# Two hybrid layers put in order by an older cost clock, and products that share the TensorE array issued with the last-ready operand first

## The chip, the cores and the metric

The kernel runs on one core of a Trainium2 chip. The metric is the device time of one execution in microseconds (us); less is better. The engines are PE (TensorE, whose weight loads are listed as PEld), DVE (VectorE), ACT (ScalarE), POOL (GpSimd) and SP (SyncE, which here issues the loads of the weights).

## What is computed

The reference passes 512 tokens of width 1024 through one block of RWKV-7 and S5 mixing with a gated feed-forward net, and then through two hybrid layers. Only the hybrid layers matter here. Cut to the core:

```
for l in range(2):
    h = rms_norm(x, norm_g)
    q_lat, kv_lat, k_rope, g_mla, c_h, c_b, c_c, g_conv, s_q, s_k, s_v, g_swa = split(h @ w_in)
    q = rms_norm(q_lat) @ w_qb               # MLA: 8 heads of 64 + 32 (the 32 with rope)
    k, v = rms_norm(kv_lat) @ w_kvb
    y_mla  = softmax(causal(q . k)) @ v * silu(g_mla)
    y_conv = c_b * conv3(c_c * c_h) * silu(g_conv)
    # 8 query heads, 2 key heads, window of 128, a slope and a sink for each head
    y_swa  = softmax(window(s_q . s_k) - slope * dist, sink) @ s_v * silu(g_swa)
    x = x + concat(y_mla, y_conv, y_swa) @ w_out
```

## The kernel before

Three parts follow one another on the core: the front (RWKV and S5), the feed-forward net, and the two hybrid layers, which take from about 838 us to the end: layer 0 to about 1215 us, layer 1 after it.

The large products are made in float32 precision from fp32r halves: each operand is split into `hi` (ACT, a copy to fp32r) and `lo` (the rest, DVE or POOL), and each product tile takes three matmuls, hi x hi, lo x hi and hi x lo. In the rows these are `mm<-hhi,whi`, `mm<-hlo,whi` and `mm<-hhi,wlo` where the input of the layer is multiplied, and `mm<-yhi,whi` and so on for `w_out`. `wraw` is a weight tile as it was loaded, `whi` and `wlo` are its halves. Small products and all transposes (`rp<-c,...`, against the identity in `c`) are of type float32.

Each layer is written as a set of Python generators, one for each strand of work: `mla_q`, `mla_k` and `swa_q` for queries and keys, `mla_s` to `mla_t` for MLA's scores, softmax and transposed probabilities (`P` in rows, `pt` in the layout for the value product), `mla_v` for the value products into `O`; `swa_s`, `swa_m`, `swa_e` and `swa_v` for the window attention (`P`, transposed into `wt`); `gated` multiplies `O` with the gate into `yt` and splits it into `yhi` and `ylo`. `sums` (L2207) adds squares for the key and query norms: four products with 32 columns of the array each (`rp<-sq,c`), one on each quarter of it, and four transposes of the result. Two products of 64 columns (`O<-pt,vt` and `O<-wt,vs`) also share the array, one for each head of a pair.

A scheduler, class `Flow`, runs while the kernel is built. At each step it asks every strand for its next operation, works out when that could start (`look`) and, from a cost model (`cost`), when its engine is free again, and issues the one with the least start time plus a bias for its strand (`turn`, `run`). `emit` issues it on the line L541, which is therefore the line of all operations that no helper issues, transposes among them. So the model's figures set the order of each engine's instructions; on the chip each engine works through its own list in that order and waits for operands by semaphores. The model has a table of latencies from engine to engine (`AFTER`), a price for changing between float32 and fp32r products on PE (`SWITCH`), and a rule that an operation of DVE with two SBUF operands and one of POOL do not run together (`ported`). The order in which weight loads stand on SP's queue comes from job lists, in the order of the products. `over` (in the body) is called when the last products of the feed-forward net have been issued, and starts the first hybrid layer.

Of the kernel before, what the change touches and what calls it, by code (L numbers as in the profile page):

```python
# [14 lines left out]
PSUM = bass.MemoryType.PSUM  # L15
# [362 lines left out]
class Flow:  # L378
# [9 lines left out]
    SWITCH = 0.06  # L388

    def __init__(self, tc):  # L390
        self.tc = tc
        self.free, self.log, self.slot, self.count = {}, {}, {}, {}
        self.live, self.now, self.last, self.beside = [], 0.0, {}, set()
        self.kind, self.ports = None, {"DVE": [], "Pool": []}
        self.table, self.psum = None, set()
        self.part, self.recent, self.ticks, self.urgent, self.late = None, [], {}, lambda: False, lambda: False
# [36 lines left out]
    def cost(eng, fn, out, args, kw=None):  # L433
        kw = kw or {}
        size = lambda ap: int(np.prod([c for _, c in ap.ap[1:]]))
        n, name = size(out), getattr(fn, "__name__", "")
        if eng == "PE":
            ins = [a for a in args if hasattr(a, "ap")]
            n, m = size(ins[-1]), size(ins[1])
            if ins[1].dtype == F32R:  # L440
                return (max(n, m) + 32) / 2400.0
            if name == "transpose":
                return n * 2 / 2400.0
            return 4 * max(n, m) / 2400.0
        psum = Flow.psums(args, kw)
        if eng == "ACT":
            return max(0.19, (0.165 if psum else 0.195) + n * 0.00085) + sum(
                c for k, c in (("accum_out", 0.19), ("bias", 0.08), ("scale", 0.08)) if hasattr(kw.get(k), "ap"))
        if name in ("reduce_sum", "tensor_reduce"):
            n = size(kw.get("in_", out))  # L450
        if eng == "DVE":
            rate = 2.0 if name == "tensor_tensor_scan" else 0.5 if not psum and name in ("TS", "memset", "tensor_copy") else 1.0
            return 0.15 + n * rate / 960.0 + (0.06 if n > 50 and (name == "tensor_tensor_reduce" or name in ("TS", "STT") and hasattr(args[2], "ap"))
                                              else 0.0)
# [5 lines left out]
    def ported(eng, fn, args, kw):  # L460

        name = getattr(fn, "__name__", "")
        if eng not in ("DVE", "Pool") or name in ("memset", "dma_start"):
            return False
# [22 lines left out]
    def look(self, o):  # L487
# [9 lines left out]
        for (key, p0, p1, f0, f1), w in boxes:  # L497
            for q0, q1, g0, g1, t, w2, e2 in self.log.get(key, ()):
                if (w or w2 or e2 != eng and key in self.psum) and p0 < q1 and q0 < p1 and f0 < g1 and g0 < f1:
                    if eng == "PE" and e2 == "PE" and (w and w2):  # L500
                        continue
                    start = max(start, t + (0.95 if e2 == "DMA" else self.AFTER.get((e2, eng), 0.2)))
        if not dma and self.ported(eng, fn, args, kw):
# [34 lines left out]
    def emit(self, o, plan):  # L538
# [11 lines left out]
        if eng == "PE":  # L550
            kind = args[1].dtype == F32R
            start, self.kind = start + (self.SWITCH if self.kind not in (None, kind) else 0.0), kind
        end = start + self.cost(eng, fn, out, args, kw) if not dma else start + (0.1 if eng != "Pool" else 1.05)
# [1356 lines left out]
class Layer:  # L1910
# [296 lines left out]
    def sums(self, ts, cols):  # L2207

        X, R, o = self.X, self.R, Flow.op
        ps = yield from R["rp"].take()  # L2210
        for j, t in enumerate(ts):
            yield o(X.MM, ps[32 * j:32 * j + 32], cols, t)
        R["sq"].free(*ts)
# [242 lines left out]
    def mla_v(self):  # L2456
        X, R, o, M = self.X, self.R, Flow.op, self.mla
        for h in range(0, 8, 2):
            yield lambda: 7 + h // 2 in self.gates
            O = yield from R["O"].take()  # L2460
            for c in range(4):
                yield lambda: ("t", h, c) in M and ("t", h + 1, c) in M
                for e in range(2):
                    pt, n, g = M.pop(("t", h + e, c)), (4 - c) * 128, (h + e) * 64
# [86 lines left out]
    def swa_v(self):  # L2551
        X, R, o, M = self.X, self.R, Flow.op, self.mla
        for pr in range(4):
            O = None
            for hf in range(2):
# [20 lines left out]
                for n, (qb, c) in enumerate(blocks):  # L2576
                    for e in range(2):
                        yield o(X.MM, O[64 * e:64 * e + 64, qb * 128:(qb + 1) * 128], self.vs[:, c, e * 64:(e + 1) * 64],
# [278 lines left out]
def second(X, top, tail, stop):  # L2857
# [21 lines left out]

    def over():  # L2880
        fst.close()
        lp, R["lt"], yp = [pool(top, n) for n in ("lp", "lt", "ly")]
# [39 lines left out]
```

## Time and profile before

| what | value |
| --- | --- |
| three runs | 1603.16, 1604.68, 1603.89 us (median 1603.89) |
| profiled execution | 1600.54 us, its span 1598.8 us |
| PE busy | 1505.8 us, 94% of the span |
| DVE, ACT, POOL busy | 868.5, 656.3, 531.0 us |
| granted TensorE clock, mean | 0.982 |

Busy means that an instruction of the engine was running. The span is the time from the first to the last instruction in the trace; the execution's own time is 1.7 us longer. In rows, `out<-in` names the output and input tiles, `xN` says how many instructions were taken together, and brackets say how long the engine had been idle ahead of the row and what released it.

### The profile page before, as it was taken

Reading aid. Unit: us, or ns where it says so; the run is one execution under the profiler, and the core shown is the slowest. Engines: PE = TensorE matmul, PEld = TensorE weight load, DVE = VectorE, ACT = ScalarE, POOL = GpSimd, SP = SyncE. Lnnn points to the kernel's source line nnn. Section 1 sums busy time; section 2 is a strip of 40 time slices with the busy share of each in tenths; the row PEclk is TensorE's granted clock in tenths of the full one; section 3 lists DMA queues with packets and bytes.
Section 4 is the critical chain, followed back from the end, with each engine's and each line's share of the span. In section 5 each row is a group of like instructions: output and inputs, shape, how many; then the busy total and the mean of one; then the engine's idle time right before and its main releaser. Section 6 shows DMA issues by size and latency. Waiting matters only on the chain. (4 is left out here: it accounts for less than half of the span.)

```text
span 1598.8 us, 23587 instructions
## 1 busy us (share of the span) xinstructions
PE 1505.8 (94%) x8772; PEld 1134.7 (71%) x8772; DVE 868.5 (54%) x2011; ACT 656.3 (41%) x1316; POOL 531.0 (33%) x498
## 2 busy tenths in 40 slices
PE   4998999998879999999999999999989999999988
PEld 2666677675458888888888777776768867766766
DVE  6858875784774222222234753547855574354872
ACT  3422533231243333333333664464544555355451
POOL 1111341221333333334433454522233454532221
PEclk9999999999989999999999999999989999999999
DMA  6773141323122322333322212221112312211212
GB/s 246 288 206 82 55 112 31 115 52 94 57 78 81 99 93 99 100 91 96 101 90 83 73 47 66 81 71 54 60 53 71 105 59 67 80 60 54 73 47 86
DMA packets 97684, 141.92 MB, mean 89 GB/s; under 512 B 40977, under 2 KB 44945, under 8 KB 97553
## 3 DMA queue, kind: packets, MB, share of 16 engines
q1 hardware_dynamic: 90512, 120.46, 24.9%
q0 software_dynamic: 5760, 18.88, 3.8%
q8 instruction: 69, 1.13, 0.3%
q10 hardware_dynamic: 1296, 1.07, 0.2%
q14 instruction: 47, 0.38, 0.1%
HBM read 135.39 MB, written 4.98 MB: 88 GB/s over the span
## 5 line engine op out<-in xcount | busy, mean ns | idle before, releaser
L236 POOL TENSOR_TENSOR wlo<-wraw,whi 128x512 fp32r<-128x512 f32 (+2 forms) x300 | 376.9, 1258 | 753.0 <-ACT whi L233 731.2
L233 ACT ACTIVATE whi<-wraw 128x512 fp32r<-128x512 f32 (+2 forms) x392 | 239.6, 613 | 448.8 <-PE mm L255 315.4
L255 PE MATMUL mm<-hhi,whi 128*128 128x512 f32 x920 | 369.8, 402 | 3.9 <-ACT vt L233 2.1
L255 PE MATMUL mm<-hhi,wlo 128*128 128x512 f32 x920 | 369.6, 402 | 3.3 <-DVE wlo L236 1.5
L255 PE MATMUL mm<-hlo,whi 128*128 128x512 f32 x920 | 368.3, 400 | 0.0
L255 PEld LDWEIGHTS mm<-hhi,wlo 128*128 128x128 f32 x920 | 175.6, 191 | 45.7 <-POOL wlo L236 4.2
L255 PEld LDWEIGHTS mm<-hhi,whi 128*128 128x128 f32 x920 | 175.4, 191 | 45.6 <-issue 7.2
L255 PEld LDWEIGHTS mm<-hlo,whi 128*128 128x128 f32 x920 | 175.7, 191 | 41.3 <-issue 6.1
L236 DVE TENSOR_TENSOR wlo<-wraw,whi 128x512 fp32r<-128x512 f32 (+1 forms) x92 | 64.7, 703 | 112.9 <-ACT whi L233 112.8
L255 PE MATMUL mm<-yhi,whi 128*128 128x512 f32 x224 | 92.8, 414 | 5.3 <-ACT yhi L233 5.3
L255 PE MATMUL mm<-ylo,whi 128*128 128x512 f32 x224 | 91.1, 407 | 1.7 <-POOL ylo L236 1.7
L255 PE MATMUL mm<-yhi,wlo 128*128 128x512 f32 x224 | 90.6, 405 | 0.0
L255 PE MATMUL mm<-ahi,whi 128*128 128x512 f32 x176 | 69.3, 394 | 0.0
L255 PE MATMUL mm<-ahi,wlo 128*128 128x512 f32 x176 | 69.0, 392 | 0.0
L255 PE MATMUL mm<-alo,whi 128*128 128x512 f32 x176 | 68.3, 388 | 0.0
L541 PEld LDWEIGHTS rp<-c,P 128*128 128x128 f32 x272 | 32.5, 140 | 36.6 <-issue 14.0
L541 DVE CUSTOM_DVE_ANT_0 P<-rp,c,nsq 128x128 f32<-128x128 f32 (+1 forms) x64 | 34.1, 550 | 43.2 <-PE rp L255 29.7
L236 DVE TENSOR_TENSOR xres<-xres,mm 128x512 f32<-128x512 f32 x48 | 32.7, 685 | 45.4 <-PE mm L255 45.1
L541 PE MATMUL rp<-c,P 128*128 128x128 f32 x272 | 47.4, 282 | 10.5 <-DVE P L249 10.3
L252 DVE SCALAR_TENSOR_TENSOR xres<-mm,ada,xres 128x512 f32<-128x512 f32 x40 | 29.7, 748 | 48.3 <-PE mm L255 48.0
L255 PEld LDWEIGHTS mm<-yhi,whi 128*128 128x128 f32 x224 | 43.2, 193 | 15.5 <-ACT yhi L233 6.5
L252 DVE SCALAR_TENSOR_TENSOR g<-th,mm 128x512 f32<-128x512 f32 x21 | 14.5, 688 | 70.5 <-PE mm L255 70.5
(548 smaller groups left out, 2656.7 us busy)
## 6 DMA issues: line engine op xcount, KB each, us to landing
wraw<-in_w2m SPq DMA_DIRECT2D x124, 256.0 KB, 2.7
wa<-in_wada SPq DMA_DIRECT2D x40, 512.0 KB, 5.1
wraw<-in_wo SPq DMA_DIRECT2D x48, 256.0 KB, 2.7
wraw<-in_wgate SPq DMA_DIRECT2D x44, 256.0 KB, 2.7
wraw<-in_wup SPq DMA_DIRECT2D x44, 256.0 KB, 2.8
wraw<-in_wdown SPq DMA_DIRECT2D x40, 256.0 KB, 2.7
wraw<-in_wz POOLq DMA_DIRECT2D x24, 256.0 KB, 3.2
wa<-in_wada POOLq DMA_DIRECT2D x8, 512.0 KB, 3.5
```

The costliest lines, as they stand in the source:

```text
L233: return self.act.activation(out=out, in_=in_, func=func, **kw)
L236: return (eng or self.dve).tensor_tensor(out=out, in0=a, in1=b, op=op)
L252: return self.dve.scalar_tensor_tensor(out=out, in0=a, scalar=s, in1=b, op0=op0, op1=op1)
L255: return self.pe.matmul(out, lhsT=lhsT, rhs=rhs, start=start, stop=stop)
L541: ins = fn(*args, **kw)
```

## The change

No instruction is added or taken out: each engine has as many as before, and SP's queue is the same. What differs is the order on PE, DVE, ACT and POOL, from the point at which `over` is called; the front and the feed-forward net up to there are as before. (1) `over` sets `Flow.rough`: from there the model uses a second table of latencies, `ROUGH`, an fp32r product without the 32 columns added, shorter ACT and DVE operations, no price for changing between float32 and fp32r, and no port rule. (2) `sums` issues its four products in reverse, the last operand first. (3) `mla_v` and `swa_v` issue the second head of a pair (`e` = 1) ahead of the first.

```diff
+    ROUGH = {("PE", "ACT"): 0.2, ("PE", "DVE"): 0.24, ("ACT", "DVE"): 0.15, ("DVE", "ACT"): 0.14, ("DVE", "DVE"): 0.125,
+             ("ACT", "ACT"): 0.2, ("DVE", "PE"): 0.2, ("ACT", "PE"): 0.25, ("PE", "PE"): 0.04}
+    rough = False
...
             if ins[1].dtype == F32R:
-                return (max(n, m) + 32) / 2400.0
+                return (max(n, m) + (0 if Flow.rough else 32)) / 2400.0
...
+        if Flow.rough and eng == "ACT":
+            return max(0.11, 0.06 + n * 0.00087) + sum(
+                c for k, c in (("accum_out", 0.1), ("bias", 0.12), ("scale", 0.08)) if hasattr(kw.get(k), "ap"))
...
+        if Flow.rough and eng == "DVE":
+            half = 0.5 if name in ("TS", "memset") or name == "tensor_copy" and "PSUM" not in str(args[1].tensor.space) else 1.0
+            return 0.067 + n * half / 960.0 + (0.06 if n > 50 and (name == "tensor_tensor_reduce" or name in ("TS", "STT") and hasattr(args[2], "ap"))
+                                               else 0.0)
...
-        if eng not in ("DVE", "Pool") or name in ("memset", "dma_start"):
+        if Flow.rough or eng not in ("DVE", "Pool") or name in ("memset", "dma_start"):
             return False
...
-                    start = max(start, t + (0.95 if e2 == "DMA" else self.AFTER.get((e2, eng), 0.2)))
+                    start = max(start, t + (0.95 if e2 == "DMA" else (self.ROUGH if Flow.rough else self.AFTER).get((e2, eng), 0.2)))
...
-            start, self.kind = start + (self.SWITCH if self.kind not in (None, kind) else 0.0), kind
+            start, self.kind = start + (self.SWITCH if self.kind not in (None, kind) and not Flow.rough else 0.0), kind
...
-        for j, t in enumerate(ts):
-            yield o(X.MM, ps[32 * j:32 * j + 32], cols, t)
+
+        for j in reversed(range(len(ts))):
+            yield o(X.MM, ps[32 * j:32 * j + 32], cols, ts[j])
...
                 yield lambda: ("t", h, c) in M and ("t", h + 1, c) in M
-                for e in range(2):
+
+                for e in (1, 0):
...
                 for n, (qb, c) in enumerate(blocks):
-                    for e in range(2):
+                    for e in (1, 0):
...
     def over():
+        Flow.rough = True
```

Three places show the new order. First PE in the first `sums` of layer 0; `rp_8023` (after: `rp_8026`) is the sum's tile, `kb` rows are transposes of MLA's keys. Before:

```order
L255 MATMUL rp_8023<-sq_7887,c_4357 32x512
L255 MATMUL rp_8023<-sq_7915,c_4357 32x512
L255 MATMUL rp_8023<-sq_7991,c_4357 32x512
L255 MATMUL mm_8007<-hhi,whi_7943 128x512
L255 MATMUL mm_8007<-hlo,whi_7943 128x512
L255 MATMUL mm_8007<-hhi,wlo_7944 128x512
...
L255 MATMUL rp_8023<-sq_8009,c_4357 32x512
L255 MATMUL mm_8007<-hhi,whi_7972 128x512
```

After:

```order
L255 MATMUL mm_8002<-hhi,wlo_7945 128x512
L553 MATMUL rp_7862<-c_68,yt_7842 128x128
L255 MATMUL rp_8026<-sq_8004,c_4357 32x512
L255 MATMUL rp_8026<-sq_7988,c_4357 32x512
L255 MATMUL rp_8026<-sq_7919,c_4357 32x512
L255 MATMUL rp_8026<-sq_7891,c_4357 32x512
L553 MATMUL rp_8040<-c_68,kb_8028 128x128 x4
L255 MATMUL mm_8002<-hhi,whi_7968 128x512
```

The six fp32r products that stood between the third and the fourth product of the sum (three of them are left out above) have moved, and the four stand in one piece.

Second, DVE at the end of layer 1: the softmax of the last half of the last head pair of the window attention (`wmn` its maximum, `wse` and `wrs` its sum, `P` the probabilities). Before:

```order
L236 TENSOR_TENSOR gate_13961<-mm_13860,rb 128x512
L541 TENSOR_REDUCE wmn<-sc_13819 128x4
L252 SCALAR_TENSOR_TENSOR gate_13961<-sq_13977,gate_13961 128x512
L236 TENSOR_TENSOR xres<-xres,mm_13960 128x512
L236 TENSOR_TENSOR wmn<-wmn,nsink 128x4
L236 TENSOR_TENSOR wmn<-wmn,c_4357 128x4
L236 TENSOR_TENSOR wse<-wmn,rows 128x4
L236 TENSOR_TENSOR wrs<-wrs,wse 128x4
L541 RECIPROCAL wrs<-wrs 128x4
L249 TENSOR_SCALAR P_14025<-P_14025,wrs 128x256 x4
```

After:

```order
L553 TENSOR_REDUCE wmn<-sc_13781 128x4
L236 TENSOR_TENSOR wmn<-wmn,nsink 128x4
L236 TENSOR_TENSOR wmn<-wmn,c_4357 128x4
L236 TENSOR_TENSOR wse<-wmn,rows 128x4
L252 SCALAR_TENSOR_TENSOR yt_13944<-O_13905,gate_13886 128x512
L236 TENSOR_TENSOR wrs<-wrs,wse 128x4
L553 RECIPROCAL wrs<-wrs 128x4
L249 TENSOR_SCALAR P_13948<-P_13948,wrs 128x256 x4
L236 TENSOR_TENSOR gate_13992<-mm_13885,rb 128x512
L252 SCALAR_TENSOR_TENSOR gate_13992<-sq_13996,gate_13992 128x512
```

The two steps of the gate and the addition to `xres` have moved from the middle of the softmax to behind it, and `yt` of the pair before has come into it.

Third, PE at the same place, from the last transposes of `P` to the first product with the last pair's `yhi`. Before:

```order
L255 MATMUL mm_14007<-yhi_13925,whi_13943 128x512
L255 MATMUL mm_14007<-ylo_13926,whi_13943 128x512
L255 MATMUL mm_14007<-yhi_13925,wlo_13944 128x512
L541 MATMUL rp_14039<-c_68,P_14025 128x128 x4
L541 MATMUL rp_14046<-c_68,P_14025 128x128 x4
L255 MATMUL O_13988<-wt_14044,vs 64x128
L255 MATMUL O_13988<-wt_14051,vs 64x128
...
L255 MATMUL mm_14007<-yhi_14063,whi_13943 128x512
L255 MATMUL mm_14007<-ylo_14064,whi_13943 128x512
```

After:

```order
L255 MATMUL O_14005<-wt_13975,vs 64x128
L553 MATMUL rp_14013<-c_68,P_13948 128x128 x4
L553 MATMUL rp_14020<-c_68,P_13948 128x128 x4
L255 MATMUL mm_13991<-ylo_12159,whi_13888 128x512
...
L255 MATMUL mm_13991<-yhi_12943,wlo_13889 128x512
L255 MATMUL O_14005<-wt_14025,vs 64x128
L255 MATMUL O_14005<-wt_14018,vs 64x128
...
L255 MATMUL mm_13991<-yhi_13151,whi_13888 128x512
...
L255 MATMUL mm_14050<-yhi_13953,wlo_13933 128x512
L255 MATMUL mm_14050<-yhi_14043,whi_13932 128x512
```

Of the 17 products `mm` that stood ahead of the transposes of `P`, 5 now stand between them and the value products `O`, and 12 between `O` and the first product with `yhi` of the last pair, where none stood. Layer 0 ends in the same way.

## Rows read from the trace of the kernel before

**Rows 1.** The page: busy us of each engine, share of the span, instructions.

```profile
PE 1505.8 (94%) x8772; PEld 1134.7 (71%) x8772; DVE 868.5 (54%) x2011; ACT 656.3 (41%) x1316; POOL 531.0 (33%) x498
```

**Rows 2.** Stretches of 50 us: busy time by engine, granted clock, DMA share, GB/s.

```profile
1550.00:1598.80 48.80, 39.33 (x176) 30.26 (x174) 14.90 (x27) 10.62 (x23) 10.31 (x8) 0.92 0.25 82
sum 748.80, PE 713.32 PEld 539.16 DVE 414.50 ACT 360.57 POOL 279.68; mean PE 47.55 PEld 35.94 DVE 27.63 ACT 24.04 POOL 18.65
```

**Rows 3.** Waits of all engines, 838 to 1599 us: total, times, longest.

```profile
PEld O L255 <- ACT pt L233: 11.6, 35, 1.1
PE rp L541 <- DVE P L249: 10.3, 6, 3.2
...
PE mm L255 <- ACT yhi L233: 5.3, 4, 1.5
...
PE rp L541 <- POOL kb L236: 3.8, 2, 1.9
...
PE mm L255 <- ACT vt L233: 2.1, 2, 1.1
...
PE mm L255 <- POOL ylo L236: 1.7, 2, 0.8
```

**Rows 4.** PE's timeline, first `sums` of layer 0: start us, duration us.

```profile
900.76 1.23 PE L255 MATMUL rp<-sq,c 128*32 128x512 f32 x6
901.92 0.50 PE L255 MATMUL mm<-hhi,whi 128*128 128x512 f32 x1
902.27 0.40 PE L255 MATMUL mm<-hlo,whi 128*128 128x512 f32 x1
902.51 0.40 PE L255 MATMUL mm<-hhi,wlo 128*128 128x512 f32 x1
...
903.53 1.04 PE L255 MATMUL rp<-sq,c 128*32 128x512 f32 x2
904.50 0.50 PE L255 MATMUL mm<-hhi,whi 128*128 128x512 f32 x1
```

**Rows 5.** PE's timeline: a pair of MLA value products of 512 columns.

```profile
936.53 1.60 PE L255 MATMUL O<-pt,vt 128*64 128x512 f32 x4
938.06 0.55 PE L541 MATMUL rp<-c,P 128*128 128x128 f32 x3
```

**Rows 6.** The weight load of that pair's second half.

```profile
937.06 0.19 PEld L255 LDWEIGHTS O<-pt,vt 128*64 128x64 f32 x2 [0.33 <-ACT pt L233]
```

**Rows 7.** PE's timeline: a single window-attention product between fp32r products.

```profile
1515.75 0.43 PE L255 MATMUL O<-wt,vs 128*64 128x128 f32 x2
1516.11 0.50 PE L255 MATMUL mm<-yhi,wlo 128*128 128x512 f32 x1
```

**Rows 8.** Busy time by engine, layer 0, four us behind `kb`'s transposes.

```profile
928.00:932.00 4.00, 3.91 (x11) 2.77 (x10) 2.06 (x3) 2.39 (x6) 3.26 (x3) 0.60 0.21 66
```

**Rows 9.** PE's timeline at the end of layer 1.

```profile
1550.83 0.50 PE L255 MATMUL mm<-ylo,whi 128*128 128x512 f32 x1
...
1558.22 1.23 PE L541 MATMUL rp<-c,P 128*128 128x128 f32 x8 [3.17 <-DVE P L249]
...
1563.65 0.79 PE L255 MATMUL mm<-yhi,whi 128*128 128x512 f32 x1 [1.52 <-ACT yhi L233]
```

**Rows 10.** DVE's timeline at the same place.

```profile
1549.26 1.21 DVE L541 TENSOR_REDUCE wmn<-sc 128x4 f32<-128x1024 f32 x1
...
1552.99 0.69 DVE L236 TENSOR_TENSOR xres<-xres,mm 128x512 f32<-128x512 f32 x1 [1.78 <-PE mm L255]
1553.60 1.18 DVE L236 TENSOR_TENSOR wmn<-wmn,nsink 128x4 f32<-128x4 f32 x1
...
1557.40 0.16 DVE L236 TENSOR_TENSOR wrs<-wrs,wse 128x4 f32<-128x4 f32 x1 [2.23 <-ACT P L233]
```

**Rows 11.** POOL's timeline at the same place.

```profile
1553.47 1.28 POOL L236 TENSOR_TENSOR wlo<-wraw,whi 128x512 fp32r<-128x512 f32 x1 [1.09 <-ACT whi L233]
```

**Rows 12.** DVE by line and form, 900 to 1600 us: busy us, mean ns.

```profile
L236 DVE TENSOR_TENSOR wmn<-wmn,nsink 128x4 f32<-128x4 f32 x16 | 11.4, 711 | 0.3
```

More of the change, by code (lines that the diff above doesn't have):

```diff
@@ L388 @@
     SWITCH = 0.06
+    ROUGH = {("PE", "ACT"): 0.2, ("PE", "DVE"): 0.24, ("ACT", "DVE"): 0.15, ("DVE", "ACT"): 0.14, ("DVE", "DVE"): 0.125,
+             ("ACT", "ACT"): 0.2, ("DVE", "PE"): 0.2, ("ACT", "PE"): 0.25, ("PE", "PE"): 0.04}
+    rough = False
     def __init__(self, tc):
         self.tc = tc
+        Flow.rough = False
         self.free, self.log, self.slot, self.count = {}, {}, {}, {}
```

## The prediction

> **What bounds the kernel now.** First the page's busy times: PE is busy for 1505.8 us, 94% of the span [rows 1], and no other engine for more than 54%. So only time in which PE stands or works slowly can be won. Then the stretches of 50 us: from 850 us to the end, which is nearly all of the two hybrid layers, PE is busy for 713.3 of 748.8 us; 35.5 us are idle. The poorest of these stretches is the end of layer 1, with 39.33 of 48.8 us busy and a granted clock of 0.92 [rows 2]. After that the waits, to see who is waited for: the value products' weight loads wait for `pt` (11.6 us in 35 waits), PE's transposes for `P` on DVE (10.3 in 6), products for `yhi` (5.3 in 4), for `kb` (3.8 in 2), `vt` (2.1 in 2) and `ylo` (1.7 in 2) [rows 3]. Last, the timeline at those places, for what stands behind each wait. Weights are not late: no wait for a transfer is among these, and SP's queue does not change.
>
> **The change, part by part.** The work is the same, so the sum has only waits, pieces that do not share the array, and changes between products of the two types.
>
> *The sums.* Three 32-column products together start at 900.76, and the next product follows at 901.92: 1.16 us. The fourth by itself, 903.53 to 904.50, takes 0.97 [rows 4]. Three cost about as much as one, so the fourth could go with them for nothing. Around the single piece two changes of type are paid as well: the product after it is followed in 0.35 us (901.92 to 902.27) and a plain one in 0.24 (902.27 to 902.51) [rows 4], which is 0.11 more on leaving; I take 0.1 on entering too. That makes 1.1 to 1.2 us for each of six sums, or 6.6. In the new order all six go in one piece. But the piece now starts with the square that was made last, and what hides that square's eviction is fewer products; I take 5, with bounds of 2 and 6.6.
>
> *MLA's value products.* Of a pair of 512 columns the first half starts at 936.53, and what follows the second starts at 938.06: 1.53 us [rows 5]. The second half's weights wait 0.33 us for `pt` from ACT [rows 6]. A ready pair would need about 1.0 to 1.16, by the sums. There are 32 pairs, and the waits for `pt` come to 11.6 us [rows 3]; that is the upper bound. In the new order the half that is ready last goes first, and one or two products `mm` stand ahead of it, so the pair starts together. ACT's eviction ends no earlier, so most of the wait only changes its place. I take 0.14 us for each of the 24 larger pairs, 3.4 in all, nearer to zero than to 11.6.
>
> *Window attention's value products.* Eight times in the two layers a 64-column product stands alone between `mm` (half of a pair cut off); one starts at 1515.75, and the next `mm` at 1516.11: 0.36 us [rows 7]. With 0.1 for the change back, and less what it would take beside its partner (about 0.13, a guess from a third of 0.36), that is 0.33 each. In the new order none stands alone: 2.6 us.
>
> *Start of MLA in each layer.* `vt` (2.1) and `kb` (3.8) [rows 3] are waits of PE. In the new order the keys' norm is finished on DVE without other work between its steps, and `kb` transposes come some 12 us earlier and apart from each other (one such is ahead of the first sum's squares in the order shown). Both waits go, 5.9 us. Behind the two groups of `kb` transposes, between which PE stood 1.9 us, the products of the next four us ran at a mean granted clock of 0.60, that is in part at 1.2 in place of 2.4 GHz [rows 8]; 0.4 x 4 = 1.6 us are lost there, and, if layer 1 does likewise, 3.2 in all. Walking through the new order with durations of the trace, I find new waits of about 0.7, 0.4, 0.8 and 0.5 us per layer, at squares and at `P`, that is 4.8 in all. 5.9 + 3.2 - 4.8 = 4.3; I take 4, with bounds of 0 and 9.1.
>
> *End of MLA's values.* PE waits for `yhi` and then for `ylo` of the last MLA pair right behind its value products. Of `yhi`'s 5.3 us, 1.52 at the end of each layer belong to the window attention [rows 3, 9], so 1.1 per layer are here, and 0.85 for `ylo`. Seven products, at 0.24 each 1.7 us, now stand between. I take 1.4 per layer, 2.8 in all, with bounds of 0 and 3.9.
>
> *Ends of the layers.* This is the largest. From 1550.83, where the value products of the first half are done, to 1563.65, where the first product with the last `yhi` starts, are 12.82 us [rows 9]. PE has 17 `mm` there (17 x 0.24 = 4.1), the transposes (1.2) and the value products (about 1.0): 6.5 us of the 12.8 are lost. The order of DVE says why: between the maximum, which ends at 1550.47, and the next step of the same softmax at 1553.60 lie 3.1 us of gate and `xres` (with a wait of 1.78 for PE), and that step took 1.18 us where the same form took 0.16 a little later [rows 10], because POOL's `wlo` ran from 1553.47 to 1554.75 [rows 11]. In the new order the gate and `xres` come behind the softmax, so it is ready up to 4.1 us earlier; `yt`, which comes into it, fits into the 2.23 us in which DVE waits for ACT [rows 10]. The 17 `mm` go behind the transposes: 5 cover the eviction into `wt`, and 12 (2.9 us) the way from `O` to `yhi` that now costs 1.52. So transposes start 7.4 - 4.1 = 3.3 us after 1550.83, and the 17 `mm`, transposes and value products take about 6.0 to 6.3 from there: 9.4 in place of 12.8. The maximum itself may come later or earlier by what precedes it, so the bounds are 1 and 6.5; I take 3.6 for each layer, 7.2 in all.
>
> *What the coarser clock spoils.* It counts a DVE operation of 512 elements as 0.60 us where the row has 0.69 [rows 10], and a change of type as nothing. In the new order PE changes type 312 times after `over` in place of 284. 28 changes at about 0.1 are 2.9 us. For late operands: the walk found 2.4 us of new waits in the 120 us at the start of a layer. At that rate the other 260 us of each layer would have 5.2, 10.4 for both; I take half, 5, since the old order has waits in the same places that go. The lower bound is nothing, the upper twice the rate, 21. Together 8.
>
> The Trainium skill, in "TensorEngine Tiling (Array Packing)", section Key Properties, says that tiles work independently and that a change of tiling mode drains TensorE. The single pieces here agree with the first. The second speaks against the 28 additional changes; the 0.11 us on leaving a single piece may be such a drain, but no row here shows what PE does in it.
>
> The sum: -5 - 3.4 - 2.6 - 4 - 2.8 - 7.2 + 8 = -17.0 us. The profiled execution had 1600.54 us, so 1583.5; the median of the runs is 3.35 higher, which gives **1587 us**.
>
> **Rivals.** A change of 0.2%, 3.2 us, is about what a measurement can tell from none.
>
> *Only the shared products gain.* The waits at starts and ends move without shrinking: on DVE the maximum comes that much later, or a wait for `P` grows by the 17 products no longer ahead of it (4.1 us, just what the softmax gains). Then -5 - 3.4 - 2.6 + 2.9 = -8, or 1596. For it: the longest wait of the layers hangs on a chain DVE, ACT, DVE [rows 10] whose operations stay. Against it: 3.1 us are plainly foreign to that chain.
>
> *No change that shows.* Late operands cost the upper bound, 21, in place of 5: -1, or 1603. For it: 35.5 us of idle time in 749 [rows 2] is little, and an order made with latencies and durations that are off can lose as much. Against: the walked stretches have less.
>
> *Slower.* The new clock no longer keeps DVE's operations with two SBUF operands away from POOL's. A hit costs 1.02 us (1.18 against 0.16) [rows 10]. Of the 16 steps of this form about 8 or 9 are hit already (mean 711 ns) [rows 12]: (711 - 160) x 16 / 1020 = 8.6. The softmax chain has three more steps of that size in each of 16 quarters. It decides from 17 more hits on the chain that ends PE's waits; with 24 it is 1587 + 24 = 1611. The Trainium skill ("SBUF — State Buffer", section "SBUF: two separate sides") calls the port pair of DVE and GpSimd an exclusive lock that one holds for its whole instruction; the rows agree (1.18 us, and POOL's instruction ends at 1554.75). Against it: the old order, made with the rule, has hits in half of these steps anyway, and in the new one the last softmax step no longer waits for a product of PE, so it will less often coincide with a `wlo` released late.
>
> **How the numbers follow.** The forecast: 0.55, with its own range 1577 to 1594 (the end-of-layer term between 1 and 6.5 per layer, late operands between 0 and 10). Only the shared products: 0.17. No change: 0.12. Slower: 0.16. Faster by over 0.2% (below 1600.7) is the first two, 0.72; within, 0.12; slower (above 1607.1), 0.16. The range goes from 1570, where nearly all upper bounds of the gains would meet, to 1606, which holds the first three cases and leaves out most of the slower one.
>
> **What would show it.** In the changed kernel's profile: `rp<-sq,c` as x8 in one row, six times; no `O<-wt,vs` x2 between `mm`; the wait of weight loads for `pt` well below 11.6 us; waits for `kb` and `vt` gone; from the last `P` transposes to the first product with the last `yhi` some 6 us, with 17 `mm` between; busy PE in 1150 to 1200 and in the last 50 us up, or these ends earlier. It would be wrong if PE's waits for `P` stay at 10 us or grow, if `wmn<-wmn,nsink` rises towards 1 us on average, or if many short new waits for `whi`, `wlo` and `sq` add up to over 15 us.

## The result and the profile after

The changed kernel takes 1561.41 us (median of 4 runs, 1558.71 to 1563.81) against 1603.53 us before: a ratio of 0.9739, with a 95% interval of 0.9718 to 0.9761, 42 us less. The forecast was 1587 us with a range of 1570 to 1606; the direction was right, the size by far too small, and the time lies below the range. The profiled execution took 1560.24 us, 40.3 less than the one before; the account below is made against it.

The page of the changed kernel answers to [rows 1]:

```profile
PE 1469.8 (94%) x8772; PEld 1123.0 (72%) x8772; DVE 860.4 (55%) x2011; ACT 653.4 (42%) x1316; POOL 533.5 (34%) x498
```

PE is as busy as before in its share, and busy for 36.0 us less with the same 8772 instructions. So nine tenths of the gain is time in which PE counted as busy. (A group that shares the array counts as busy while one member works and another is still waited for; `e6` below shows what that hides.) The sum that was forecast looked for the larger part in waits. Where the busy time went is seen from PE's groups in the layers (busy us and mean ns of one, then idle time ahead and what ended it; the line L541 is L553 in the changed kernel, and L609 or L610 in some of the runs). Before:

```profile
L255 PE MATMUL O<-pt,vt 128*64 128x512 f32 (+3 forms) x128 | 36.3, 458 | 0.9 <-ACT pt L233 0.8
L255 PE MATMUL O<-wt,vs 128*64 128x128 f32 x224 | 22.3, 302 | 0.9 <-ACT wt L233 0.4
L255 PE MATMUL rp<-sq,c 128*32 128x512 f32 x48 | 13.1, 604 | 0.6 <-ACT sq L233 0.6
L541 PE MATMUL rp<-c,P 128*128 128x128 f32 x272 | 47.4, 282 | 10.5 <-DVE P L249 10.3
```

After:

```profile
L553 PE MATMUL rp<-c,P 128*128 128x128 f32 x272 | 45.3, 276 | 1.5 <-DVE P L249 1.2
...
L255 PE MATMUL O<-pt,vt 128*64 128x512 f32 (+3 forms) x128 | 24.3, 458 | 1.6 <-ACT pt L233 1.6
...
L255 PE MATMUL O<-wt,vs 128*64 128x128 f32 x224 | 15.8, 280 | 4.9 <-ACT wt L233 4.9
...
L255 PE MATMUL rp<-sq,c 128*32 128x512 f32 x48 | 6.4, 605 | 3.0 <-ACT sq L233 3.0
```

One of MLA's value products takes 458 ns in both; the group fell from 36.3 to 24.3 us because its halves now overlap. The three groups that share the array gave 12.0, 6.5 and 6.7 us, 25.2 together. (Of the window's 6.5 us some 1.7 are not sharing: in `e8`, below, where only the wait ahead of the last transposes is filled, the window's products take that much less.) A pair of 512 columns and a sum, on PE's timeline (compare [rows 5] and [rows 4]):

```profile
903.67 1.07 PE L255 MATMUL rp<-sq,c 128*32 128x512 f32 x8 [0.96 <-ACT sq L233]
904.66 0.66 PE L553 MATMUL rp<-c,kb 128*128 128x128 f32 x4
...
935.67 1.08 PE L255 MATMUL O<-pt,vt 128*64 128x512 f32 x4 [0.45 <-ACT pt L233]
936.68 0.50 PE L255 MATMUL mm<-hlo,whi 128*128 128x512 f32 x1
```

All four products of the sum take 1.0 us together, and the pair 1.01 where it took 1.53.

PE's waits in the two layers, which answer to [rows 3]:

```profile
PEld O L255 <- ACT pt L233: 12.1, 28, 0.9
...
PE mm L255 <- DVE wlo L236: 6.1, 4, 1.9
PE O L255 <- ACT wt L233: 4.9, 6, 1.5
...
PE rp L255 <- DVE mn L553: 3.7, 2, 1.8
PE rp L255 <- ACT sq L233: 3.0, 4, 1.0
PE rp L255 <- DVE wlo L236: 2.1, 1, 2.1
...
PE mm L255 <- POOL ylo L236: 1.6, 2, 0.8
PE rp L553 <- DVE P L249: 1.2, 2, 0.6
PE rp L553 <- POOL kb L236: 0.6, 2, 0.3
```

The waits for `yhi` and `vt` are gone, those for `P` and `kb` nearly so; others, for `wlo`, `wt`, `mn` and `sq`, have come in. Added up over the timeline, what PE waited in the layers fell only from 29.7 to 27.2 us.

The rest is in the large products. At the full granted clock they start 0.23 us apart. Counted over the timeline by starts (the time from one start on PE to the next, less the wait ahead of the next), from the last transposes of the front on, all large products take 527.0 us in place of 538.7, 11.7 less. Of the steps from one `mm` to the next `mm`, 59 were over 0.4 us before and 25 are now; their time over 0.233 us each fell from 12.8 to 5.5 us, 7.3 less. Of the products that stand alone between two pieces of other products (65 before, 44 now), 33 took 0.40 us or more before, 0.44 on average, and now none takes over 0.34; over 0.32 us each that was 3.9 us.

The granted clock tells where the long steps stood (it is the number ahead of the last two; 0.50 is the lower level, 1.2 GHz). The ends of layer 0 and of layer 1, and the start of MLA in layer 1, before:

```profile
1174.00:1185.00 11.00, 9.26 (x36) 6.75 (x35) 3.65 (x7) 3.62 (x6) 0.00 (x0) 0.53 0.09 24
1560.00:1567.00 7.00, 5.38 (x22) 3.96 (x22) 2.67 (x4) 1.41 (x3) 0.00 (x0) 0.52 0.00 1
1309.00:1317.00 8.00, 7.00 (x24) 5.26 (x25) 3.69 (x6) 4.82 (x12) 6.63 (x7) 0.79 0.15 42
```

After, the end of layer 0, the last 50 us (0.92 in [rows 2]), and the start of MLA in layer 1:

```profile
1140.00:1200.00 60.00, 56.94 (x302) 45.32 (x301) 36.24 (x72) 30.65 (x63) 24.90 (x19) 1.00 0.27 79
1508.50:1558.50 50.00, 42.43 (x217) 32.95 (x215) 20.56 (x33) 13.91 (x30) 12.90 (x10) 1.00 0.30 95
1274.00:1284.00 10.00, 7.91 (x28) 5.88 (x29) 5.99 (x15) 7.33 (x19) 2.95 (x2) 0.66 0.23 79
```

The lower clock is gone from the ends of the layers, and has grown at the start of MLA.

DVE at the end of layer 1, against [rows 10]:

```profile
1510.49 1.21 DVE L553 TENSOR_REDUCE wmn<-sc 128x4 f32<-128x1024 f32 x1
1511.74 0.98 DVE L236 TENSOR_TENSOR wmn<-wmn,nsink 128x4 f32<-128x4 f32 x1
...
1515.77 3.18 DVE L249 TENSOR_SCALAR P<-P,wrs 128x256 f32<-128x256 f32 x4
```

From the maximum's end to the next step it is 0.04 us in place of 3.1. That step still takes 0.98 us, as it meets an operation of POOL (`wlo`, 1511.41 to 1512.69), and the four steps on `P` took 3.18 us, where before they took 1.14, with two more operations of POOL beside them:

```profile
1515.92 1.33 POOL L236 TENSOR_TENSOR ylo<-yt,yhi 128x512 fp32r<-128x512 f32 x1 [3.23 <-ACT yhi L233]
1517.21 1.31 POOL L236 TENSOR_TENSOR wlo<-wraw,whi 128x512 fp32r<-128x512 f32 x1
```

And PE there, against [rows 9]:

```profile
1517.45 0.66 PE L553 MATMUL rp<-c,P 128*128 128x128 f32 x4
1518.73 0.70 PE L553 MATMUL rp<-c,P 128*128 128x128 f32 x4 [0.62 <-DVE P L249]
...
1521.23 1.09 PE L255 MATMUL O<-wt,vs 128*64 128x128 f32 x16 [0.63 <-ACT wt L233]
```

The transposes now wait 0.62 us in place of 3.17, and the 17 products fill the rest as the order said.

### The profile page after: what moved, and what is told of

The parts are those of the page before. It is cut to its first block, busy times and chain, and to the rows that moved or that the text cites. A ratio compares the mean times of both kernels' runs of the same rounds, so it can differ in the third digit from the quotient of the medians.

```text
span 1558.5 us, 23572 instructions
## 1 busy us (share of the span) xinstructions
PE 1469.8 (94%) x8772; PEld 1123.0 (72%) x8772; DVE 860.4 (55%) x2011; ACT 653.4 (42%) x1316; POOL 533.5 (34%) x498
## 4 chain that ended last, share of the span: by engine, by line
PE 74%; DVE 15%; ACT 4%; issue 2%; DMA 2%; POOL 1%; SPq 0%; ACTq 0%; DVEq 0%; POOLq 0%
PE mm L255 54%; PE rp L255 10%; PE rp L553 2%; PE O L255 2%; PE rq L255 2%; PE acc L255 2%; PE cz L255 1%; DVE wlo L236 1%; DVE sc L236 1%; DVE sq L236 1%; DVE P L249 1%; DVE qp L236 1%; POOL wlo L236 1%; DVE cy L252 1%; ACT qp L233 1%
## 5 line engine op out<-in xcount | busy, mean ns | idle before, releaser
L236 DVE TENSOR_TENSOR wlo<-wraw,whi 128x512 fp32r<-128x512 f32 (+1 forms) x92 | 73.9, 804 | 113.7 <-ACT whi L233 102.9
L553 DVE CUSTOM_DVE_ANT_0 P<-rp,c,nsq 128x128 f32<-128x128 f32 (+1 forms) x64 | 34.2, 549 | 45.4 <-PE rp L255 41.3
L252 DVE SCALAR_TENSOR_TENSOR xres<-mm,ada,xres 128x512 f32<-128x512 f32 x40 | 29.7, 747 | 48.3 <-PE mm L255 48.1
L252 DVE SCALAR_TENSOR_TENSOR th<-th,mm 128x512 f32<-128x512 f32 x20 | 13.7, 687 | 69.9 <-ACT th L233 69.9
L236 DVE TENSOR_TENSOR xres<-xres,mm 128x512 f32<-128x512 f32 x48 | 32.5, 681 | 35.0 <-PE mm L255 34.8
L255 PEld LDWEIGHTS mm<-ylo,whi 128*128 128x128 f32 x224 | 42.1, 188 | 12.5 <-POOL ylo L236 2.3
L255 PEld LDWEIGHTS mm<-yhi,wlo 128*128 128x128 f32 x224 | 42.0, 188 | 10.1 <-issue 1.1
```

The lines of the kernel that those rows point to most:

```text
L236: return (eng or self.dve).tensor_tensor(out=out, in0=a, in1=b, op=op)
L252: return self.dve.scalar_tensor_tensor(out=out, in0=a, scalar=s, in1=b, op0=op0, op1=op1)
L255: return self.pe.matmul(out, lhsT=lhsT, rhs=rhs, start=start, stop=stop)
L553: ins = fn(*args, **kw)
```

## The experiments

Each run was timed against the kernel before on the same chip; the medians of before lay between 1600.4 and 1604.3 us, and differences here are taken within a run. Theory A: the groups that share the array give 25 us by which member is issued first. Its rival B: they give the 11 us of the forecast, and the order made by the older clock (the second set of figures, which `Flow.rough` turns on) the rest.

**The two parts apart.** `e1` is the changed kernel without `Flow.rough`, `e2` the changed kernel with the three loops as before:

```diff
     def over():
-        Flow.rough = True
```

> The old clock, with only the reversed order of the sums and of the two value products. Theory A (about 25 us of the 42 come from products that now share the array, whatever clock orders the rest): 1576 to 1584 us, value products of MLA near 22 us and those of the window near 15 us of PE time. Theory B (the shared products are worth the 11 us of the forecast, and the older clock's order brings the rest): 1590 to 1595 us.

Measured: 1572.14 us, ratio 0.9821 (0.9800 to 0.9841).

> The older clock, with the sums and the value products issued in the order of before. Theory A: 1583 to 1592 us, MLA's value products still at 32 to 36 us of PE time. Theory B: 1570 to 1577 us.

Measured: 1570.17 us, ratio 0.9811 (0.9790 to 0.9832). Each part alone gives 30 us, and both together 42. In `e1` the three groups fell to the same 24.3, 15.8 and 6.4 us as in the changed kernel; in `e2` they stayed at 34.8, 20.0 and 13.2, as A said, and yet its time is what B said. Neither theory holds as it stood: `e1` is faster than both allowed, and the older clock's order does much by itself, and what it does overlaps with what the other part does. In both most of the wait for `P` at the layers' ends went (10.3 to 2.2 and to 1.7 us; in `e2` the same transposes wait 4.3 us for `sc`, the scores, instead).

**One group put back.** `e3` and `e4` are the changed kernel with one loop as before (here that of `e3`; `e4` turns the same line in `swa_v`):

```diff
-                for e in (1, 0):
+                for e in (0, 1):
                     pt, n, g = M.pop(("t", h + e, c)), (4 - c) * 128, (h + e) * 64
```

> The changed kernel with MLA's value products alone put back to the first head first. Theory A: 12 us longer than the changed kernel, about 1573 us. Theory B: 3 to 4 us longer, about 1565 us.

Measured: 1588.22 us, ratio 0.9916 (0.9895 to 0.9937).

> The changed kernel with the window attention's value products alone put back to the first head first. Theory A: 6 us longer than the changed kernel, about 1567 us, with single products between the large ones again. Theory B: 2 to 3 us longer, about 1564 us.

Measured: 1561.98 us, ratio 0.9758 (0.9742 to 0.9774). The window's products went back to 20.7 us of busy time, 4.9 more, and the time did not: with 0.5 us less of waits for `wt` and 14 steps between large products over 0.4 us in place of 25, it cost nothing that can be told. MLA's cost 27 us, more than twice what A allowed. The waits of `e3` tell why this can't be read as the price of the pair:

```profile
PE rp L553 <- DVE P L249: 11.0, 14, 1.2
PE mm L255 <- DVE wlo L236: 6.5, 4, 2.0
```

The wait for `P` is back, in the window attention, which the edit does not touch: one loop turned round gives the scheduler other start times, and it makes another order for all that follows.

**The same edit with every place kept.** So the choices of the scheduler (which strand comes next, 5411 times after `over`) were written down and played back; a loop can then be turned round while everything else stays where it was:

```diff
+            if Flow.mark:
+                best = next(x for x in ready if x[1][3] == PICKS[Flow.picked])
+                Flow.picked += 1
             what, best[1][1] = best[1][1], None
```

Theory C is that `e3`'s loss is the pair's own.

> The changed kernel, with every instruction kept in its place by a list of the scheduler's choices; only the two halves of each of MLA's 32 value pairs change places. Theory A (the pair itself is worth 12 us; what e3 lost beyond that came from the other order which the scheduler then made, with the wait for the last softmax back): 9 to 13 us above the changed kernel, 1570 to 1574 us, and no wait for P. Theory C (e3's loss is the pair's: it is worth 27 us): 1585 to 1590 us.

Measured: 1557.99 us, ratio 0.9732 (0.9711 to 0.9753), the same as the changed kernel. A fell, and so did C: with its place kept, it makes no difference which half goes first. The other way round, in the kernel before:

> The kernel before, with every instruction kept in its place; only the two halves of each of MLA's value pairs change places. Theory A: PE's time in these products falls from 34 to 22 us, and since fewer products stand ahead of the pair than in the changed kernel, 3 to 5 us of waits for pt come in: 7 to 10 us below the kernel before. By the forecast's step (the wait only changes its place): 2 to 4 us below.

Measured: 1597.77 us against 1600.39, ratio 0.9989 (0.9977 to 1.0001): 2.6 us, which is not clear of none. PE's groups and waits in `e6`:

```profile
L255 PE MATMUL O<-pt,vt 128*64 128x512 f32 (+3 forms) x128 | 24.3, 458 | 10.3 <-ACT pt L233 10.0
```

The halves overlap as in the changed kernel, 12.0 us less; and 9.2 us more are waited for `pt` (0.8 before). That is the forecast's sentence, that the wait only changes its place, in numbers; it is true of the edit that it was said of.

From this came theory D: issuing the last operand first helps by what the scheduler does with it. It starts an operation when its operands are there; if the first of a group needs the last operand, the whole group is put off until then, and other work comes ahead of it.

> The changed kernel, every instruction kept in its place, with the sums, MLA's and the window's value products all issued first operand first again, as in the kernel before. Theory D (issuing the last operand first does not help PE; it makes the scheduler wait with all products of a group until the last operand is there, so that they stand together with other products ahead of them): 1556 to 1564 us, no more than 4 us above the changed kernel. Theory A (which of a group goes first on PE is what counts): 1572 us or more.

Measured: 1557.18 us, ratio 0.9736 (0.9717 to 0.9754). D held where A gave 1572 or more: all three groups first operand first again, at the places of the changed kernel, and the time is the same. The groups:

```profile
L255 PE MATMUL O<-pt,vt 128*64 128x512 f32 (+3 forms) x128 | 26.2, 458 | 0.0
L255 PE MATMUL O<-wt,vs 128*64 128x128 f32 x224 | 18.2, 281 | 2.5 <-ACT wt L233 2.0
L255 PE MATMUL rp<-sq,c 128*32 128x512 f32 x48 | 9.6, 605 | 0.0
```

They are up to 3.2 us longer each, because the members that are ready work while the last is waited for, and the waits are as much shorter.

**The place alone.** In the kernel before, by list, first head first: `e13` puts the two products that followed each of the 32 pairs ahead of it.

> The kernel before, every instruction kept in its place as far as it can be, and the value pairs with the first head first as before; only that of the products which followed each of MLA's 32 value pairs the next two now stand ahead of it. Theory D (what gains is that other products stand ahead of a pair until its last operand is there): PE's time in these products falls from 34 to 22 to 25 us with no more than 4 us of waits for pt, 8 to 11 us below the kernel before. If the wait only changes its place here too: less than 4 us below.

Measured: 1604.72 us, ratio 1.0011 (0.9998 to 1.0024). D's number was missed. The pairs fell only to 31.2 us of busy time, and the products taken from behind them were missing there: the transposes of both heads now stood side by side. By starts, from the front's last transposes on, the pairs took 5.2 us less, but the transposes 2.9 us more (44.6 to 47.5), the waits 1.7 more, and the large products, the scores and the window's products 2.0 more together. It was the wrong place. In the changed kernel the pair also has the transposes of the next block's first head ahead of it; `e15` moves 24 of the 32 pairs (all with a further block behind them) to there and nothing else. On PE, in words: `P` of the second head, one product, `P` of the next block's first head, one product, pair; before, the pair came ahead of the last two.

> The kernel before, first head first as before; only 24 of MLA's 32 value pairs stand one step later on PE, behind the transposes of the next block's first head and one product, as they stand in the changed kernel. If the transposes of the next block are the cover that e13 lacked: PE's time in the pairs falls from 34 to 22 to 26 us, transposes and products stay at 45 and 538, and the time is 8 to 11 us below the kernel before. If the pair's place is worth nothing by itself: within 3 us of it, as e13.

Measured: 1596.39 us against 1604.28, ratio 0.9952 (0.9937 to 0.9968), 8 us below the kernel before. The first pairs of `e15`:

```profile
939.98 0.49 PE L610 MATMUL rp<-c,P 128*128 128x128 f32 x3
940.23 0.47 PE L255 MATMUL mm<-hlo,whi 128*128 128x512 f32 x1
940.63 1.08 PE L255 MATMUL O<-pt,vt 128*64 128x512 f32 x4
941.64 0.55 PE L610 MATMUL rp<-c,P 128*128 128x128 f32 x3
```

The pair takes 1.01 us with the first head first and no wait ahead of it; the group fell to 26.5 us. So the pair's place is worth about 8 us by itself (5 to 10 by the interval), and the next block's transposes are the cover that `e13` lacked. (The expectation that transposes and `mm` would stay at 45 and 538 us failed in part: by starts, `mm` rose from 538.7 to 541.8 us, with 4.4 us more in steps over 0.4 us, and the transposes by 1.0. That execution, the slowest of the four of `e15`, had the lower clock for longer at the end of layer 1, where the edit moves nothing: 0.54 over 15 us, from 1553 to 1568 us, where the kernel before had 0.52 over 7.)

**The end of the layers.** By list, in the kernel before, DVE's three small steps directly behind the maximum of each layer's last softmax.

> The kernel before, with every instruction kept in its place, except that in the last softmax of each layer DVE's three small steps stand directly behind the maximum, ahead of the gate and of xres. If the foreign steps are what is late there: the two waits of 3.2 us for P go, and with them most of the slow products behind them, 7 to 10 us below the kernel before. If the chain's own steps set it: less than 3 us.

Measured: 1592.52 us against 1600.39, ratio 0.9956 (0.9942 to 0.9970), 7 to 8 us. DVE and PE of `e7`:

```profile
1543.04 1.20 DVE L610 TENSOR_REDUCE wmn<-sc 128x4 f32<-128x1024 f32 x1
1544.28 0.16 DVE L236 TENSOR_TENSOR wmn<-wmn,nsink 128x4 f32<-128x4 f32 x1
```

```profile
1550.08 1.23 PE L610 MATMUL rp<-c,P 128*128 128x128 f32 x8 [1.25 <-DVE P L249]
```

The softmax step takes 0.16 us, and PE waits 1.25 us where it waited 3.17. The foreign steps were what was late; the waits for `P` fell from 10.3 to 6.5 us and did not go altogether.

> The run before this one together with the softmax steps moved as in e7. If the two are separate: the sum of their gains, 15 to 18 us below the kernel before, 1582 to 1586 us. If they draw on the same idle time: 10 us or less.

Measured: 1593.43 us against 1602.71, ratio 0.9940 (0.9923 to 0.9957), 9 us. `e13` gave nothing to add, so this tells no more than `e7`.

> The run before this one with the softmax steps moved as in e7. If the two add up: 15 to 19 us below the kernel before, 1583 to 1587 us, which is over a third of the change with no rule of the clock changed. If they draw on the same idle time: 7 to 10 us.

Measured: 1585.15 us against 1604.28, ratio 0.9881 (0.9865 to 0.9898), 19 us. The two add up (8 and 8), and what is over lies within the interval (16 to 22 us). Two moves by hand in the old order give some 45% of the change; the rest was not reproduced by moves of this kind.

**The clock of the products.** In `e8`, in the kernel before and by list, 12 products more fill the wait ahead of the last transposes of each layer.

```diff
+                    if (pr, hf, e) == (3, 1, 0):
+                        hi = self.ys[0, 0][0]
+                        for _ in range(12):
+                            f = o(X.MM, ps, hi[:, 0:128], hi)
+                            X.flow.emit(f, X.flow.look(f))
```

> The kernel before, with every instruction kept in its place; ahead of the last transposes of P in each layer PE makes 12 more fp32r products, whose result is overwritten, in the 3.2 us in which it stands. If standing is what lowers the granted clock behind it: the products after these two places run at 0.23 us from start to start again, 3 to 5 us below the kernel before although it does more. If the clock falls for another reason: no change, or up to 1 us longer.

Measured: 1596.32 us against 1600.39, ratio 0.9971 (0.9956 to 0.9986): 4 us less for 5.8 us of more work. PE of `e8` at the end of layer 1:

```profile
1551.39 2.88 PE L255 MATMUL rp<-yhi 128*128 128x512 f32 x12
1554.74 1.23 PE L610 MATMUL rp<-c,P 128*128 128x128 f32 x8 [0.47 <-DVE P L249]
1556.19 1.61 PE L255 MATMUL O<-wt,vs 128*64 128x128 f32 x16 [0.22 <-ACT wt L233]
1559.32 0.50 PE L255 MATMUL mm<-yhi,whi 128*128 128x512 f32 x1 [1.52 <-ACT yhi L233]
```

The same stretch by its granted clock:

```profile
1554.74:1564.00 9.26, 7.20 (x42) 5.24 (x43) 3.78 (x8) 2.94 (x5) 0.00 (x0) 1.00 0.16 44
```

The clock behind the place is 1.00, where it was 0.52 before, and the first product lasts 0.50 us in place of 0.79 [rows 9]. By starts, in both layers, all large products took 4.9 us less, and the window's value products 1.7. So standing still is what makes PE slow there, beyond the wait itself.

**Parts of the older clock.** All with the groups issued last operand first, as in `e1` (1572, no part) and the changed kernel (1561, all). Theory F is that the shorter durations are what counts. One of the three places that `e10` edits:

```diff
-                    start = max(start, t + (0.95 if e2 == "DMA" else (self.ROUGH if Flow.rough else self.AFTER).get((e2, eng), 0.2)))
+                    start = max(start, t + (0.95 if e2 == "DMA" else self.AFTER.get((e2, eng), 0.2)))
```

> Groups issued last operand first, and of the older clock only the durations of the operations; latencies, the price of a change of type and the port rule as before. Theory D (no one part of the clock holds the gain; each clock makes an order with other waits): between 1559 and 1575 us. Theory F (the shorter durations are what counts): 1561 us as the changed kernel, and the next run 1572 us as the one with the old clock.

Measured: 1571.30 us, ratio 0.9820 (0.9806 to 0.9835).

> Groups issued last operand first, and of the older clock only the latencies from engine to engine. Theory D: between 1559 and 1575 us. Theory F: 1572 us. If the latencies are what counts: 1561 us here and 1572 us in the run with durations alone.

Measured: 1599.33 us, ratio 0.9986 (0.9971 to 1.0001).

> The changed kernel, with the port rule and the price of a change of type kept for the layers. If leaving these two out is what gains: 1568 to 1573 us. If it is what the older clock loses by (hits at the port): 1552 to 1557 us. If they matter little beside the rest: 1559 to 1564 us.

Measured: 1568.88 us, ratio 0.9800 (0.9771 to 0.9828). F fell (durations alone gain nothing over `e1`), and so did the one for latencies, which alone lose 27 us. D's range failed for `e11` too, which lies far outside. The waits at its top:

```profile
PE rp L553 <- POOL kb L236: 8.2, 4, 3.0
PE rp L553 <- DVE P L249: 7.3, 7, 2.5
PE mm L255 <- ACT yhi L233: 4.5, 3, 1.5
```

The waits of the kernel before are all back in `e11`, for `kb`, `P` and `yhi`, although its groups stand together. Each set of figures makes an order of its own. That leaving out the port rule and the price of a change of type is worth 7 to 10 us beside the rest (1569 against 1561) is what `e12` shows, in this one order; its four runs lie 10 us apart (1562 to 1573).

## Why the prediction was wrong

The forecast failed at two steps: it took the pairs' gain for a wait that only moves, and it put the lower clock in the large products at the ends of the layers at nothing.

*The sums* were right: 6.7 us less busy, 2.4 more waited for squares, 4.3 net, where 5 stood in the sum.

*MLA's value products* are the first step that failed. The forecast saw that a pair took 1.53 us and would take 1.0 to 1.16, which it does (1.01), and put the bound at 11.6 us. It then took 3.4, since the wait would only change its place. `e6` shows that this is so (2.6 us) if the two halves are swapped and nothing else; but in the changed kernel the pairs also stand elsewhere, behind the next block's transposes, and the group gave 12.0 us for 0.8 us more of waiting. `e15` shows the place's share, 8 us. The forecast had the new order and named products ahead of the pair, and did not price them as cover. Its bound came near by luck: it was read from the waits of the weight loads for `pt`, and these did not fall (11.6 to 12.1 us), against the sign that was named, though the pairs overlap.

*The window's products* fell by 6.5 us, and the waits for `wt` rose by 4.5: 2.0 net, forecast 2.6; `e4` finds nothing that can be told from none.

*Start of MLA* won no 4 us. The waits for `kb` and `vt` fell from 5.9 to 0.6 as forecast, but the new ones are larger than the walk found: `mn` 3.7, `sq` 1.9 at the first sums, and two for `wlo` of 1.9 and 1.4, 8.9 in place of 4.8. The 3.2 us for the lower clock did not come either: priced as the forecast does, (1 - clock) x time, 1.7 us were lost there in layer 1 before (0.79 over 8 us) and 3.4 are now (0.66 over 10 us, in 1.4 of which PE stood).

*End of MLA's values*: `yhi` went, 2.2 of the 2.8 us forecast; `ylo` is as late as before (1.6).

*Ends of the layers*: the waits for `P` and `yhi` gave 9.1 and 3.0 us, 12.1; the new waits for `wt`, which were already taken off at the window's products, stand here, so that it is 7.6 if they are taken off here instead; forecast 7.2 (its own 12.8 less 9.4 makes 3.4 for each layer and not 3.6). The stretch that the forecast walked, from the end of the first half's value products to the first product with the last `yhi`, took 7.7 us in layer 1 (1517.45 to 1525.16) in place of 12.8. `e7` shows the mechanism, with 7 to 8 us of its own.

*What the coarser clock spoils* was put at 8 us; the new waits in the layers (`wlo` 4.6 and 2.1 more, `mn` 3.7, `wt` 4.5, `sq` 3.1 more at two places, `pt` 0.8) are 18.8, part of which the steps above had. All waits together fell by 2.5 us. The forecast held a drain at a change of tiling mode against the 28 additional changes, which are changes of type: before, the first `mm` behind float32 transposes on the whole array was followed after 0.32 us on average, and behind 32-column pieces after 0.34, so that at most 0.02 of the 0.11 us can belong to the tiling.

*The lower clock* is the second step that failed. The sum had 3.2 us for it, at the start of MLA, where it did not go; at the ends of the layers, where it went, the sum had nothing. Priced in the same way, 5.2 us were lost at the end of layer 0 (0.53 over 11 us) and 3.4 at the end of layer 1 (0.52 over 7 us), 8.6 together, or 7.1 without the 1.5 us in each in which PE stood for `yhi`; 1.7 of these were in the value products, inside the stretch that the forecast walked, and none is lost there now. The profile showed this before: 0.92 in the last stretch of [rows 2], 0.79 us for a product in [rows 9]. Steps between large products over 0.4 us gave 7.3 us, single products 3.9, and all large products 11.7 by starts; why the single ones are quicker was not tried. `e8` shows for the place at the end of each layer what the long steps are: waiting costs twice, once while PE stands, and again in the products behind.

So of the 23 us between the forecast and the profiled execution's 40.3, the pairs are 8 (12.0 less 0.8 of waiting and the 3.4 counted) and the large products about 8 (11.7 less 3.2) more than was counted; the rest is spread over smaller differences and was not tried one by one. The range was also drawn too narrow for its own terms: the upper bounds of the gains (6.6, 11.6, 2.6, 9.1, 3.9 and 13.0 us) less 2.9 for changes of type make 43.9, which is 1560 and not 1570.

Of the rivals, that only the shared products gain (1596) missed by the same term. The slower one had a true mechanism: in the new order `P` of the last softmax took 3.18 us in place of 1.14 beside two operations of POOL. But the step `wmn<-wmn,nsink` fell from 711 to 314 ns on average, against [rows 12], so hits at the port grew fewer in one place and cost 2 us in another. Ten of the 16 steps of this form ran beside a `wlo` or `ylo` of POOL before (the forecast worked out 8 or 9), and four do now; each of these ended within 0.03 us behind POOL's operation. The Trainium skill ("SBUF — State Buffer", section "SBUF: two separate sides") gives the port pair of DVE and GpSimd to whichever starts first, for its whole instruction. The trace agrees: all 14 ended right behind POOL's. What stays open is why the older figures order the layers better: the durations alone add nothing to `e1`, the latencies alone do harm, and the port rule and the price of a change of type were not left out by themselves.

## What to carry to other kernels

Here, products that share the array overlapped fully (1.01 us for a pair in place of 1.53) when all their operands were there at the start of the first. So look for groups that take clearly longer than one member, and price the gain by the full overlap once enough other work stands ahead of the group (`e15` had it, `e13` not). A wait on PE can cost more than its length: look at the granted clock of the products behind it, at each place by itself. Which member goes first matters little by itself; in a list scheduler it matters because it tells the scheduler when the group can go. One turned loop can shift every later decision: to learn what an edit is worth, hold the order and change that edit alone.

## What the runs showed of the hardware

The value products at the end of layer 1 in the kernel before, on PE's timeline:

```profile
1559.67 2.45 PE L255 MATMUL O<-wt,vs 128*64 128x128 f32 x16 [0.22 <-ACT wt L233]
```

Filling a wait with products that nobody needs made the kernel 4 us faster (`e8`): these 16 then took 1.61 us in place of 2.45, and the first large product 0.50 in place of 0.79, with PE at its higher clock (granted 1.00 in place of 0.52). In before, the stretch behind the transposes of `kb` had a granted clock of 0.60 [rows 8], so part of the time was at 1.2 GHz. The lower clock also followed a shorter wait: in `e7`, behind one of 1.25 us and one of 1.52 us within five us, the stretch from 1556 to 1562 us had 0.72.
